# One feed-forward of layer 0 for the latent and the context tokens together

## The chip, the cores and the metric

The kernel runs on one core of a Trainium2 chip. The metric is the device time of one execution in microseconds (us). The engines are PE (TensorE, with its weight loads listed as PEld), DVE (VectorE), ACT (ScalarE), POOL (GpSimd) and SP (SyncE, which here issues most transfers). Lines such as L136 are lines of the kernel before.

## The reference, cut to what matters

Two blocks run one after the other. The first has two layers over 512 latent tokens (`x`) and 256 context tokens (`ctx`), 1024 features each; the second block, with an MLP in each of its two layers, works on the latent tokens alone. In layer 0 both streams pass through the same feed-forward with the same weights; in layer 1 only the latent stream does.

```
def conv_ffn(h, w_up, dw_w, dw_b, w_down):          # D_FF = 2816
    a, u = jnp.split(h @ w_up, 2, axis=-1)
    a = depthwise_conv(a, dw_w, dw_b)               # 3 taps along the tokens
    return (jax.nn.silu(a) * u) @ w_down
...
    x = layer_norm(ALPHA * x + ml[..., 2, :] * mix(zl, attn_l), ln1_g[l], ln1_b[l])
    x = layer_norm(ALPHA * x + ml[..., 5, :] * ffn(modulate(x, ml[..., 3, :], ml[..., 4, :])), ln2_g[l], ln2_b[l])
    if not last:                                    # layer 0 only
        ...
        ctx = layer_norm(ALPHA * ctx + mc[5] * ffn(modulate(ctx, mc[3], mc[4])), ln2_g[l], ln2_b[l])
```

`ml` and `mc` are six rows each, made from the conditioning vectors by a matrix `w_ada[l]` (`ada_mod`). The rows of layer 1 are needed from the end of layer 0 on.

## The kernel before

Every fp32 operand is kept as two halves, a rounded one (`hi`) and the rest (`lo`), and each product is three matmuls: hi x hi, hi x lo, lo x hi (`mm`, L153, L154, L155). A weight **unit** is 512 KB, 128 partitions by 1024 numbers. `unit` loads it on SP's queue into one of three `raw` buffers (L141), ACT rounds it into the `hi` half of a `w` buffer (L135), and DVE or POOL subtracts to get `lo` (L136). There are six `w` buffers; of every twelve units, `pool_share` go to POOL. Activations are cut in the same way by `split`, on buffers of tag `s8`.

The feed-forward (`ffn`) takes the 22 blocks of 128 hidden features, j, in three groups, (0,8), (8,16), (16,22). For each j, `up` multiplies two units (the `a` half and the `u` half) with all tokens, each into a PSUM bank of its own (tag `mm`, three banks). The activation follows: ACT copies `a` into a padded row (L1019), DVE does the three taps (L1021, L1024), ACT the tanh (L1027), DVE the products (L1028, L1029) and the cut into halves. After a group, `down` multiplies the group's features into the output tiles of 128 tokens, two halves of 512 features each. In the last group `tm_pair` finishes a tile at a time: scaling by the gate and sum (L1047 to L1049), then `ln_finish` (L581 to L600): on DVE the modulated rows h for the next stage (L591, L592, L595), and later (`residual`) on ACT and POOL the normalized rows that go to memory (L598 to L600). PE turns h into features by transposes (L310), and ACT and DVE cut them.

In layer 0, the mix of the latent stream ends with the product with `w_out` (`out_ln`) and writes its h to memory (`h_dram`, buffer `hd["l0"]`). Then the feed-forward of the context stream runs, woven with the first four of the twelve steps of `ada_vec` (rows of layer 1; DVE multiplies weight tiles with the conditioning vector, L502 and L504, and PE sums over partitions, L484; its weight tiles use `w` buffers as well); half of the units are cut on POOL (`pool_share` 6). Before its last group the latent h is read back (`reload`). The context's result goes to memory (`hd["c1"]`). Then the feed-forward of the latent stream runs, woven with the other eight steps, all units cut on DVE; its h stays on chip. The keys of layer 1 (`kv`) come next, and read the context's h back. `weave` takes steps of its generators by their rates; the order on each engine then follows a scheduler of the framework, which places instructions as their inputs and buffers are expected.

## Time and profile before

| | us |
|---|---|
| median of 3 runs | 4060.96 |
| lowest, highest | 4060.53, 4068.85 |
| the profiled execution | 4057.85 |
| its span, first to last instruction | 4056.1 |

| engine | busy, us | share of the span |
|---|---|---|
| PE | 3785.9 | 93% |
| DVE | 2729.4 | 67% |
| ACT | 1535.6 | 38% |
| POOL | 1059.9 | 26% |

The mean granted TensorE clock was 0.969 of full speed. The transfers moved 471.54 MB. A group of the profile's lines gives busy time, the mean of one instruction, and the idle time before these instructions with what ended it. Durations of neighbouring instructions overlap a little, so a pace is read from start to start.

### The profile page before, as it was taken

The page shows a single profiled execution, that of the slowest core. Times are in us where ns is not written, and L with a number is a line of the kernel's source. Part 1 is how long each engine was busy: PE and PEld are TensorE (multiplying, and loading weights), DVE is VectorE, ACT ScalarE, POOL GpSimd, SP SyncE. Part 2 cuts the span into 40 slices and gives each one's busy share as a digit, 9 for nine tenths or more (in the row PEclk, how much of TensorE's full clock was granted, in tenths as well). Part 3 has the DMA queues.
Part 4 walks back from the last instruction along what each step waited for, and adds up shares of the span by engine and source line. Part 5 has one row for each costly group of instructions (what it writes and reads, how often), then busy time and mean ns, then how long its engine had stood idle before and what let it go on. Part 6 is the DMA issues. An engine that isn't in the chain of part 4 may idle for free.

```text
span 4056.1 us, 49639 instructions
## 1 busy us (share of the span) xinstructions
PE 3785.9 (93%) x18765; PEld 3128.9 (77%) x18765; DVE 2729.4 (67%) x3713; ACT 1535.6 (38%) x2685; POOL 1059.9 (26%) x1028
## 2 busy tenths in 40 slices
PE   7788999799889999999979999999999999999999
PEld 4678787577687878777767788889788888778887
DVE  4998699976889766879996754563354346764444
ACT  3535444234343332344324233233432225653233
POOL 3654421675444001432256300110000002420000
PEclk9889999899999999999989999999999999999999
DMA  6456312355566455322234423333233232023332
GB/s 204 118 144 210 100 52 88 112 149 164 167 210 199 157 156 166 128 76 60 75 94 122 133 94 104 116 126 98 80 97 99 83 107 77 16 81 102 98 94 94
DMA packets 545242, 471.54 MB, mean 116 GB/s; under 512 B 30870, under 2 KB 435966, under 8 KB 545002
## 3 DMA queue, kind: packets, MB, share of 16 engines
q1 hardware_dynamic: 544922, 468.10, 37.5%
q8 instruction: 147, 2.41, 0.2%
q14 instruction: 93, 0.76, 0.1%
q0 software_dynamic: 80, 0.26, 0.0%
HBM read 443.50 MB, written 24.80 MB: 115 GB/s over the span
## 4 chain that ended last, share of the span: by engine, by line
PE 60%; DVE 26%; DMA 5%; issue 4%; ACT 3%; POOL 2%; SPq 0%; ACTq 0%; POOLq 0%; DVEq 0%
PE mm L153 18%; PE mm L154 18%; PE mm L155 18%; DVE s L787 10%; DVE w L136 4%; DVE s L136 2%; DVE s L504 1%; DVE st L740 1%; DMA w<-in_w_ada 1%; ACT w L135 1%; DMA raw<-in_w_in 1%; PE acc L161 1%; PE b L1256 1%; PE b L310 1%; DVE t L1024 1%
## 5 line engine op out<-in xcount | busy, mean ns | idle before, releaser
L153 PE MATMUL mm<-s,w 128*128 128x512 f32 (+1 forms) x3072 | 1126.9, 369 | 75.3 <-ACT pad L1019 19.0
L154 PE MATMUL mm<-s,w 128*128 128x512 f32 (+1 forms) x3072 | 1119.9, 365 | 10.2 <-DVE s L136 10.2
L155 PE MATMUL mm<-s,w 128*128 128x512 f32 (+1 forms) x3072 | 1117.5, 364 | 2.2 <-DVE w L136 2.2
L135 ACT CAST w<-raw 128x1024 fp32r<-128x1024 f32 (+4 forms) x673 | 689.2, 1029 | 820.0 <-PE mm L155 411.2
L136 DVE TENSOR_TENSOR w<-raw,w 128x1024 fp32r<-128x1024 f32 (+3 forms) x517 | 667.5, 1295 | 293.7 <-ACT w L135 288.8
L153 PE MATMUL mm<-w,s 128*128 128x512 f32 (+2 forms) x1960 | 750.4, 384 | 11.9 <-ACT s L135 5.6
L153 PEld LDWEIGHTS mm<-s,w 128*128 128x128 f32 x3072 | 599.8, 196 | 188.0 <-ACT pad L1019 21.2
L154 PE MATMUL mm<-w,s 128*128 128x512 f32 (+2 forms) x1960 | 741.6, 379 | 1.3 <-DVE w L136 1.3
L155 PE MATMUL mm<-w,s 128*128 128x512 f32 (+2 forms) x1960 | 739.0, 379 | 1.3 <-DVE s L136 1.3
L154 PEld LDWEIGHTS mm<-s,w 128*128 128x128 f32 x3072 | 602.0, 196 | 94.2 <-DVE s L136 12.1
L155 PEld LDWEIGHTS mm<-s,w 128*128 128x128 f32 x3072 | 600.9, 196 | 89.9 <-DVE w L136 2.6
L787 DVE SCALAR_TENSOR_TENSOR s<-pad,cols,s 128x512 f32<-128x512 f32 (+1 forms) x690 | 578.8, 881 | 1.1
L136 POOL TENSOR_TENSOR w<-raw,w 128x1024 fp32r<-128x1024 f32 (+1 forms) x156 | 420.2, 2695 | 471.6 <-ACT w L135 463.0
L153 PEld LDWEIGHTS mm<-w,s 128*128 128x128 f32 x1960 | 370.3, 189 | 92.3 <-issue 14.2
L155 PEld LDWEIGHTS mm<-w,s 128*128 128x128 f32 x1960 | 370.1, 189 | 67.6 <-DVE s L136 2.6
L154 PEld LDWEIGHTS mm<-w,s 128*128 128x128 f32 x1960 | 370.5, 189 | 63.6 <-DVE w L136 2.7
L320 POOL TENSOR_SCALAR st<-st 128x1 f32<-128x1 f32 (+2 forms) x91 | 32.8, 360 | 1216.1 <-ACT s L1086 902.4
L1101 DVE TENSOR_TENSOR s<-s,mm 128x512 f32<-128x512 f32 x80 | 54.6, 685 | 172.2 <-PE mm L155 172.2
L136 DVE TENSOR_TENSOR s<-b,s 128x256 fp32r<-128x256 f32 (+2 forms) x224 | 119.6, 545 | 51.2 <-ACT s L135 50.3
L135 ACT CAST s<-b 128x256 fp32r<-128x256 f32 (+2 forms) x224 | 104.1, 474 | 123.2 <-DVE s L136 73.4
L1117 DVE TENSOR_TENSOR t<-t 128x512 f32<-128x512 f32 x64 | 44.3, 692 | 154.0 <-ACT t L1116 154.0
L504 DVE SCALAR_TENSOR_TENSOR s<-w,cond,s 128x512 f32<-128x512 f32 x112 | 101.0, 921 | 43.4 <-DMA w<-in_w_ada 43.0
(273 smaller groups left out, 4307.2 us busy)
## 6 DMA issues: line engine op xcount, KB each, us to landing
raw<-in_w_up SPq DMA_DIRECT2D x196, 512.0 KB
raw<-in_w_in SPq DMA_DIRECT2D x180, 512.0 KB
raw<-in_w_down SPq DMA_DIRECT2D x130, 512.0 KB
w<-in_w_ada SPq DMA_DIRECT2D x48, 512.0 KB
raw<-in_w_ada SPq DMA_DIRECT2D x32, 512.0 KB
s<-d SPq DMA_DIRECT2D x26, 512.0 KB
raw<-in_conv_pw_w SPq DMA_DIRECT2D x24, 512.0 KB
raw<-in_w_out SPq DMA_DIRECT2D x24, 512.0 KB
```

The costliest lines, as they stand in the source:

```text
L135: self.nc.scalar.copy(hi, src)
L136: (eng or self.nc.vector).tensor_sub(lo, src, hi.bitcast(F32))
L153: mm(out, lhsT=l[0], rhs=r[0], start=first, stop=False)
L154: mm(out, lhsT=l[0], rhs=r[1], start=False, stop=False)
L155: return mm(out, lhsT=l[1], rhs=r[0], start=False, stop=last)
L161: self.nc.tensor.matmul(out, lhsT=l, rhs=r, start=first and n == 0, stop=last and n == len(terms) - 1)
L310: self.pe_mark = nc.tensor.transpose(ps[:, c, :], src[:, (c0 + c) * P : (c0 + c + 1) * P], self.ident)
L504: nc.vector.scalar_tensor_tensor(out=v, in0=w, scalar=c, in1=v, op0=ALU.mult, op1=ALU.add)
L740: self.mark = nc.vector.reduce_max(out=s[:, 0:1], in_=S[:, :nkeys], axis=AX.X, negate=True)
L787: nc.vector.scalar_tensor_tensor(out=o, in0=pad[:, k : k + T], scalar=self.col("dww", 8 * k + j), in1=o, op0=ALU.mult, op1=ALU.add)
L1101: nc.vector.tensor_add(x(t)[:, cs], x(t)[:, cs], ps)
L1117: nc.vector.tensor_mul(r, r, r)
```

## The change

Layer 0 gets one feed-forward for both streams, `ffn_both`. Each unit of `w_up` and `w_down` is loaded and cut once and used for the context tokens, then for the latent tokens: 66 fewer unit loads (34.6 MB), casts and subtractions. There are six groups: (0,2), (2,6), (6,10), (10,14), (14,18), (18,22). The two products of the context share one PSUM bank (`both`); those of the latent stream have one each. `down` has six output tiles (two of the context, four of the latent stream), and the last group finishes all six, the context's first.

The latent h of the mix and the context's h at the end stay on chip (`h_feat`), so both memory buffers and both reloads go. All twelve steps of `ada_vec` are woven in, from the start, at a rate of 2; `pool_share` stays 0. For the whole kernel there are twelve `s8` buffers instead of eleven and five `w` buffers instead of six. The second layer's `ffn` now has the groups (0,9), (9,18), (18,22). `ln_prep` can share the rows g and b of another call. The activation is moved, unchanged, into `ffn_act`.

```diff
+ADAV = 2
...
-    BUFS = {"s8": 11, "s4": 6, "w": 6, "raw": 3, "t2": 4, "pad": 6, "st": 16, "row": 3, "fa": 2, "colst": 2, "br": 1}
+    BUFS = {"s8": 12, "s4": 6, "w": 5, "raw": 3, "t2": 4, "pad": 6, "st": 16, "row": 3, "fa": 2, "colst": 2, "br": 1}
...
-    def ln_prep(self, g, b, mod, gate):
-
-        nc = self.nc
-        t1 = self.sb([P, 2, D], F32, "s8")
-        gb, bb = t1[:, 0, :], t1[:, 1, :]
-        self.bcast(gb, g)
-        self.bcast(bb, b)
+    def ln_prep(self, g, b, mod, gate, like=None):
+
+        nc = self.nc
+        if like is None:
+            t1 = self.sb([P, 2, D], F32, "s8")
+            gb, bb = t1[:, 0, :], t1[:, 1, :]
+            self.bcast(gb, g)
+            self.bcast(bb, b)
+        else:
+            gb, bb = like["g"], like["b"]
...
+    def ffn_act(self, H, i, j, pa, pu, T):
+
+        nc = self.nc
+        pad = self.sb([P, T + 30], F32, "pad")
+        nc.gpsimd.memset(pad[:, 0:1], 0.0)
+        nc.gpsimd.memset(pad[:, T + 1 : T + 2], 0.0)
+        nc.scalar.copy(pad[:, 1 : T + 1], pa)
+        a = self.sb([P, 512], F32, "t2")[:, :T]
+        nc.vector.tensor_scalar(a, pad[:, 0:T], scalar1=self.col("fww", j), scalar2=self.col("fwb", j),
+                                op0=ALU.mult, op1=ALU.add)
+        for k in (1, 2):
+            nc.vector.scalar_tensor_tensor(out=a, in0=pad[:, k : k + T], scalar=self.col("fww", 22 * k + j), in1=a,
+                                           op0=ALU.mult, op1=ALU.add)
+        th = self.sb([P, 512], F32, "t2")[:, :T]
+        nc.scalar.activation(th, a, AF.Tanh, scale=0.5)
+        nc.vector.scalar_tensor_tensor(out=a, in0=th, scalar=1.0, in1=a, op0=ALU.add, op1=ALU.mult)
+        nc.vector.tensor_mul(a, a, pu)
+        self.split(H.hi(i), H.lo(i), a)
+
+    def ffn_both(self, l, parts):
+
+        nc, A = self.nc, self.A
+        groups = [(0, 2), (2, 6), (6, 10), (10, 14), (14, 18), (18, 22)]
+        ys = [self.ytiles() for _ in parts]
+        sts = [[self.st() for _ in range(p[0].nt)] for p in parts]
+        tiles = [(q, t) for q, p in enumerate(parts) for t in range(p[0].nt)]
+        gate, bc = [], []
+        W1, W2 = A["w_up"][l], A["w_down"][l]
+
+        def add_prev(q, t, cs, ps, gi):
+            S, _, _, xin, _, _ = parts[q]
+            yt = ys[q](t)
+            if gi == 0:
+                nc.scalar.copy(yt[:, cs], ps)
+                return
+            nc.vector.tensor_add(yt[:, cs], yt[:, cs], ps)
+            if gi == len(groups) - 2:
+                xt = self.sb([P, 512], F32, "t2")
+                nc.sync.dma_start(xt, xin[t * P : t * P + P, cs])
+                nc.gpsimd.tensor_mul(yt[:, cs], yt[:, cs], gate[q][:, cs])
+                nc.vector.scalar_tensor_tensor(out=yt[:, cs], in0=xt, scalar=ALPHA, in1=yt[:, cs], op0=ALU.mult, op1=ALU.add)
+
+        def finish(q, t, n, ps):
+            S, _, mod, _, xout, h_out = parts[q]
+            yt, cs = ys[q](t), slice(n * 512, n * 512 + 512)
+            if len(bc) <= q:
+                bc.append(self.ln_prep(A["ln2_g"][l], A["ln2_b"][l], mod, None, bc[0] if bc else None))
+            v = self.sb([P, 512], F32, "t2")
+            nc.vector.tensor_mul(v, ps, gate[q][:, cs])
+            nc.vector.tensor_add(yt[:, cs], yt[:, cs], v)
+            nc.vector.bn_stats(out=sts[q][t][:, 6 * n : 6 * n + 6], in_=yt[:, cs])
+            return self.ln_finish(S, yt, t, sts[q][t], bc[q], xout, h_out) if n == 1 else None
+
+        for gi, (j0, j1) in enumerate(groups):
+            nk = j1 - j0
+            Hs = [Feat(self, p[0].T, nk) for p in parts]
+            for j in range(j0, j1):
+                us = [self.unit(W1[:, c : c + P], KD, P) for c in (j * P, DFF + j * P)]
+                for (S, X, *_), H in zip(parts, Hs):
+                    T = S.T
+                    if T <= 256:
+                        both = self.ps("mm")
+                        pss = [both[:, :T], both[:, T : 2 * T]]
+                    else:
+                        pss = [self.ps("mm")[:, :T] for _ in us]
+                    for u, ps in zip(us, pss):
+                        for k in range(KD):
+                            self.mm(ps, [u.part(hl, k, 0, P) for hl in (0, 1)], (X.hi(k), X.lo(k)), k == 0, k == KD - 1)
+                    self.ffn_act(H, j - j0, j, *pss, T)
+                yield
+            if gi == len(groups) - 2:
+                for p in parts:
+                    gate.append(self.sb([P, D], F32, "s4"))
+                    self.bcast(gate[-1], self.gate_row(l, p[0].s, 1))
+            last = gi == len(groups) - 1
+
+            def product(us, q, t):
+                tk = slice(t * P, t * P + P)
+                ps = self.ps("mm")
+                for k in range(nk):
+                    u, i = us[k]
+                    self.mm(ps, (Hs[q].hi(k)[:, tk], Hs[q].lo(k)[:, tk]), [u.part(hl, i, 0, 512) for hl in (0, 1)],
+                            k == 0, k == nk - 1)
+                return ps
+
+            if not last:
+                for n in range(2):
+                    us = self.tm_units(W2, 512 * n, 512, j0, nk)
+                    for q, t in tiles:
+                        add_prev(q, t, slice(512 * n, 512 * n + 512), product(us, q, t), gi)
+                    yield
+                continue
+            us = [self.tm_units(W2, 512 * n, 512, j0, nk) for n in range(2)]
+            late = None
+            for q, t in tiles:
+                for n in range(2):
+                    f = finish(q, t, n, product(us[n], q, t))
+                self.call(late)
+                late = f
+                yield
+            self.call(late)
+        self.flush()
...
-        groups = [(0, 8), (8, 16), (16, 22)]
+        groups = [(0, 9), (9, 18), (18, 22)]
...
+                self.ffn_act(H, i, j0 + i, pa, pu, T)
...
-    mix(0, lat, Xl, kT, vs, LAT + CTX, True, net.mod_rows(0, 0, 1), x0, xd["lat", 0], h_dram(hd["l0"]),
+    Xf = Feat(net, LAT, KD)
+    mix(0, lat, Xl, kT, vs, LAT + CTX, True, net.mod_rows(0, 0, 1), x0, xd["lat", 0], h_feat(Xf),
         before_out=lambda: Xcf.append(reload(cx, xd["ctx", 0], net.mod_rows(0, 1, 1))), extra=net.ada(0, 6, 12))
     if stop == "mix0":
         return xd["lat", 0], xd["ctx", 0]
-    Xlf = []
-    net.pool_share = 6
-    weave((net.ffn(0, cx, Xcf[0], bc_of(0, cx, True), xd["ctx", 0], None, h_dram(hd["c1"]),
-                   before_last=lambda: Xlf.append(reload(lat, hd["l0"]))), 1),
-          (net.ada_vec(1, 0, 4), 0.75))
-    net.pool_share = 0
-    Xf = Xlf[0]
-    X1 = Feat(net, LAT, KD)
-    weave((net.ffn(0, lat, Xf, bc_of(0, lat, True), xd["lat", 0], xd["lat", 1], h_feat(X1)), 1),
-          (net.ada_vec(1, 4, 12), 1.25))
+    X1, Xc1 = Feat(net, LAT, KD), Feat(net, CTX, KD)
+    net.mods[1] = net.dram([2, 6, D])
+    weave((net.ffn_both(0, [(cx, Xcf[0], net.mod_rows(1, 1, 0), xd["ctx", 0], None, h_feat(Xc1)),
+                            (lat, Xf, net.mod_rows(1, 0, 0), xd["lat", 0], xd["lat", 1], h_feat(X1))]), 1),
+          (net.ada_vec(1, 0, 12), ADAV))
     if stop == "ffn0":
-        return xd["lat", 1], hd["c1"]
+        return xd["lat", 1], None
 
     net.load_cols(1)
     net.gains(1)
     kT, Vc = keys(1)
-    vs = lat_keys(1, X1, kT, Vc, reload(cx, hd["c1"]))
+    vs = lat_keys(1, X1, kT, Vc, Xc1)
```

On PE, at the end of the first context j after the mix. In the kernel before, the second product of that j (bank mm_8732) ends and the next j begins:

```order
L154 MATMUL mm_8732<-s_1299_8329,w_8704 128x256
L155 MATMUL mm_8732<-s_1299_8329,w_8704 128x256
L153 MATMUL mm_8782<-s_1298_8326,w_8774 128x256
L154 MATMUL mm_8782<-s_1298_8326,w_8774 128x256
L155 MATMUL mm_8782<-s_1298_8326,w_8774 128x256
```

The same place after the change (mm_8778 is the shared bank of the context, s_1340 the first cut features of the latent h, b_1352 and b_1353 the transposes of its last two tiles):

```order
L156 MATMUL mm_8778<-s_1297_8327,w_8775 128x256
L311 MATMUL b_1352_8711<-ident_66,s_1346_8651 128x128 x8
L311 MATMUL b_1353_8728<-ident_66,s_1351_8707 128x128 x8
L154 MATMUL mm_8842<-s_1340_8630,w_8770 128x512
L154 MATMUL mm_8843<-s_1340_8630,w_8775 128x512
L155 MATMUL mm_8842<-s_1340_8630,w_8770 128x512
```

Before, another context j follows; after, two transposes and the latent products of the same j with the same two units.

On DVE, at the same place. In the kernel before, from the normalization of the last tile of the mix (st_8670) on:

```order
L581 BN_AGGR st_8670<-st_8352 128x2
L1024 SCALAR_TENSOR_TENSOR t_1357_8761<-pad_8757,cols_343,t_1357_8761 128x256
L591 SCALAR_TENSOR_TENSOR s_1347_8674<-s_1321_8464,st_8670,s_1257_8019 128x1024
L502 TENSOR_SCALAR s_1370_8847<-w_8848,cond_88 128x512 x2
L1028 SCALAR_TENSOR_TENSOR t_1357_8761<-t_1358_8765,t_1357_8761 128x256
L592 SCALAR_TENSOR_TENSOR s_1343_8634<-s_1343_8634,st_8630,s_1257_8019 128x1024
L595 SCALAR_TENSOR_TENSOR st_8630<-st_8630 128x1
L504 SCALAR_TENSOR_TENSOR s_1370_8847<-w_8848,cond_88,s_1370_8847 128x512 x2
L1029 TENSOR_TENSOR t_1357_8761<-t_1357_8761,mm_8732 128x256
```

After the change, from the second half of that normalization (s_1351 is the last tile's h, t_1367 the first context activation, s_1376 a sum of `ada_vec`):

```order
L596 SCALAR_TENSOR_TENSOR s_1351_8707<-s_1351_8707,st_8703,s_1255_8017 128x1024
L599 SCALAR_TENSOR_TENSOR st_8703<-st_8703 128x1
L137 TENSOR_TENSOR w_8927<-raw_8925,w_8927 128x1024
L137 TENSOR_TENSOR s_1342_8636<-b_1352_8711,s_1342_8636 128x2x128
L505 SCALAR_TENSOR_TENSOR s_1376_8907<-w_8914,cond_88,s_1376_8907 128x512 x2
L1026 SCALAR_TENSOR_TENSOR t_1367_8831<-t_1368_8835,t_1367_8831 128x256
L137 TENSOR_TENSOR s_1343_8639<-b_1352_8711,s_1343_8639 128x2x128
L137 TENSOR_TENSOR s_1340_8630<-b_1353_8728,s_1340_8630 128x2x128
L1027 TENSOR_TENSOR t_1367_8831<-t_1367_8831,mm_8778 128x256
L137 TENSOR_TENSOR s_1341_8633<-b_1353_8728,s_1341_8633 128x2x128
L137 TENSOR_TENSOR s_1369_8839<-t_1367_8831,s_1369_8839 128x256
```

The cuts of the transposed latent h (b_1352, b_1353) now stand here, between the context activation and the `ada_vec` sums.

On DVE, in the last group, as a tile is finished. In the kernel before, the third latent tile (s_1783 is its sum, s_2032 to s_2035 are cut features of the tiles before it):

```order
L1047 TENSOR_TENSOR t_2037_13580<-mm_13561,s_1894_12593 128x512
L136 TENSOR_TENSOR s_2033_13552<-b_2031_13540,s_2033_13552 128x2x128
L1048 TENSOR_TENSOR s_1783_11773<-s_1783_11773,t_2037_13580 128x512
L1049 BN_STATS st_11027<-s_1783_11773 128x6
L136 TENSOR_TENSOR s_2034_13555<-b_2031_13540,s_2034_13555 128x2x128
L1047 TENSOR_TENSOR t_2039_13603<-mm_13584,s_1894_12593 128x512
L136 TENSOR_TENSOR s_2035_13558<-b_2031_13540,s_2035_13558 128x2x128
```

After the change, from the middle of the group on (s_1400 and s_1403 are pairs of latent tiles, s_1902 and s_1909 the first two latent h, w_13522 a unit for the keys):

```order
L1059 TENSOR_TENSOR t_1918_13344<-mm_13331,s_1781_12271 128x512
L595 SCALAR_TENSOR_TENSOR s_1902_13234<-s_1400_9098,st_13230,s_1896_13202 128x1024
L595 SCALAR_TENSOR_TENSOR s_1909_13289<-s_1400_9098,st_13285,s_1896_13202 128x1024
L599 SCALAR_TENSOR_TENSOR st_13230<-st_13230 128x1
L1060 TENSOR_TENSOR s_1403_9115<-s_1403_9115,t_1918_13344 128x512
L599 SCALAR_TENSOR_TENSOR st_13285<-st_13285 128x1
L137 TENSOR_TENSOR w_13522<-raw_13520,w_13522 128x1024
L1059 TENSOR_TENSOR t_1923_13386<-mm_13373,s_1781_12271 128x512
L596 SCALAR_TENSOR_TENSOR s_1902_13234<-s_1902_13234,st_13230,s_1896_13202 128x1024
```

The normalization of the first two latent tiles stands behind the products of the third, and its cut features come later than that.

## Rows read from the trace of the kernel before

**Rows 1.** Page, costliest groups: busy, mean ns, then idle before and its releasers

```profile
L155 PE MATMUL mm<-s,w 128*128 128x512 f32 (+1 forms) x3072 | 1117.5, 364 | 2.2 <-DVE w L136 2.2
L135 ACT CAST w<-raw 128x1024 fp32r<-128x1024 f32 (+4 forms) x673 | 689.2, 1029 | 820.0 <-PE mm L155 411.2
```

**Rows 2.** Windows: busy (count) of PE PEld DVE ACT POOL; clock, DMA share, GB/s

```profile
1057.00:1307.00 250.00, 215.97 (x1369) 192.76 (x1370) 229.02 (x278) 96.29 (x150) 123.19 (x93) 0.94 0.65 204
1307.00:1647.00 340.00, 336.33 (x1454) 270.91 (x1453) 230.80 (x308) 105.56 (x137) 20.24 (x56) 0.99 0.52 164
1647.00:1735.00 88.00, 80.20 (x357) 62.12 (x355) 69.36 (x119) 31.64 (x69) 41.70 (x37) 0.96 0.26 87
...
2658.00:2720.00 62.00, 58.24 (x298) 49.28 (x297) 51.68 (x83) 25.59 (x50) 11.93 (x21) 1.00 0.48 152
```

**Rows 3.** Timeline of PE: start, duration, line; first products of five stages

```profile
1056.86 0.38 PE L153 MATMUL mm<-s,w 128*128 128x256 f32 x1
...
1306.90 0.39 PE L153 MATMUL mm<-s,w 128*128 128x512 f32 x1
...
1647.44 0.39 PE L153 MATMUL mm<-w,s 128*128 128x512 f32 x1
...
1692.50 0.77 PE L153 MATMUL mm<-w,s 128*128 128x512 f32 x1
...
1735.36 0.50 PE L153 MATMUL mm<-s,w 128*128 128x512 f32 x1
```

**Rows 4.** Timeline of PE: pace of 256 and of 512 columns

```profile
1114.83 0.28 PE L153 MATMUL mm<-s,w 128*128 128x256 f32 x1
1114.95 0.28 PE L154 MATMUL mm<-s,w 128*128 128x256 f32 x1
...
1377.31 0.50 PE L153 MATMUL mm<-s,w 128*128 128x512 f32 x1
...
1399.20 0.39 PE L153 MATMUL mm<-w,s 128*128 128x512 f32 x1
```

**Rows 5.** Lines of PE, 1012 to 1320 us

```profile
L153 PE MATMUL mm<-s,w 128*128 128x256 f32 x352 | 107.7, 306 | 30.3 <-ACT pad L1019 19.0 <-DVE t L1029 8.3 <-DVE s L1063 3.0
...
L484 PE MATMUL acc<-s,ones 128*1 128x512 f32 x16 | 8.2, 591 | 3.0 <-DVE t L485 3.0
```

**Rows 6.** Lines of DVE, 1320 to 1642 us (latent feed-forward)

```profile
L136 DVE TENSOR_TENSOR w<-raw,w 128x1024 fp32r<-128x1024 f32 x60 | 72.4, 1217 | 31.8 <-ACT w L135 31.7
L504 DVE SCALAR_TENSOR_TENSOR s<-w,cond,s 128x512 f32<-128x512 f32 x56 | 41.9, 747 | 39.2 <-DMA w<-in_w_ada 38.7
L1024 DVE SCALAR_TENSOR_TENSOR t<-pad,cols,t 128x512 f32<-128x512 f32 x42 | 31.4, 748 | 1.4
...
L1029 DVE TENSOR_TENSOR t<-t,mm 128x512 f32<-128x512 f32 x21 | 14.4, 684 | 1.5
...
L1021 DVE TENSOR_SCALAR t<-pad,cols 128x512 f32<-128x512 f32 x21 | 11.3, 538 | 1.6 <-ACT pad L1019 1.6
```

**Rows 7.** Lines of DVE and POOL, 1012 to 1320 us

```profile
L136 DVE TENSOR_TENSOR s<-b,s 128x256 fp32r<-128x256 f32 x16 | 6.3, 411 | 1.7 <-ACT s L135 1.7
...
L136 POOL TENSOR_TENSOR w<-raw,w 128x1024 fp32r<-128x1024 f32 x33 | 90.4, 2740 | 77.9 <-ACT w L135 71.1 <-DMA raw<-in_w_down 6.7
```

**Rows 8.** Timelines of DVE and POOL: one operation beside POOL and alone

```profile
1062.26 2.73 POOL L600 TENSOR_TENSOR s<-s,s 128x1024 f32<-128x1024 f32 x1
...
1062.65 2.48 DVE L1021 TENSOR_SCALAR t<-pad,cols 128x256 f32<-128x256 f32 x1
...
1101.69 0.40 DVE L1021 TENSOR_SCALAR t<-pad,cols 128x256 f32<-128x256 f32 x1
```

**Rows 9.** The same stage of layer 1: last mix product, last cut, first activation

```profile
2314.77 0.50 PE L181 MATMUL mm<-br,ones 32*128 32x512 f32 x1
...
2338.48 0.42 DVE L136 TENSOR_TENSOR s<-b,s 128x256 fp32r<-128x256 f32 x1 [0.44 <-ACT s L135]
```

**Rows 10.** Timeline of DVE: end of layer 0's last normalization

```profile
1702.69 1.28 DVE L592 SCALAR_TENSOR_TENSOR s<-s,st,s 128x1024 f32<-128x1024 f32 x1
```

More of the change, by code (lines that the diff above doesn't have):

```diff
@@ L1010, in ffn @@
         y = y or self.ytiles()
-        groups = [(0, 8), (8, 16), (16, 22)]
+        groups = [(0, 9), (9, 18), (18, 22)]
         def up(H, j0, j1):
             def cb(i, pa, pu):
-                j = j0 + i
-                pad = self.sb([P, T + 30], F32, "pad")
-                nc.gpsimd.memset(pad[:, 0:1], 0.0)
-                nc.gpsimd.memset(pad[:, T + 1 : T + 2], 0.0)
-                nc.scalar.copy(pad[:, 1 : T + 1], pa)
-                a = self.sb([P, 512], F32, "t2")[:, :T]
-                nc.vector.tensor_scalar(a, pad[:, 0:T], scalar1=self.col("fww", j), scalar2=self.col("fwb", j),
-                                        op0=ALU.mult, op1=ALU.add)
-                for k in (1, 2):
-                    nc.vector.scalar_tensor_tensor(out=a, in0=pad[:, k : k + T], scalar=self.col("fww", 22 * k + j), in1=a,
-                                                   op0=ALU.mult, op1=ALU.add)
-                th = self.sb([P, 512], F32, "t2")[:, :T]
-                nc.scalar.activation(th, a, AF.Tanh, scale=0.5)
-                nc.vector.scalar_tensor_tensor(out=a, in0=th, scalar=1.0, in1=a, op0=ALU.add, op1=ALU.mult)
-                nc.vector.tensor_mul(a, a, pu)
-                self.split(H.hi(i), H.lo(i), a)
+                self.ffn_act(H, i, j0 + i, pa, pu, T)
             return self.fm_gemm(X, A["w_up"][l], [(c * P, DFF + c * P) for c in range(j0, j1)], cb, lead=1 if lead and j0 == 0 else 0)
@@ L1641, in first_block @@
     xd = {(S.name, i): net.dram([S.T, D]) for S in (lat, cx) for i in range(3)}
-    hd = {k: net.dram([S.T, D]) for k, S in (("l0", lat), ("c1", cx))}
-    def h_dram(dst):
-        def f(t, h):
-            nc.sync.dma_start(dst[t * P : t * P + P, :], h)
-        return f
     def h_feat(X):
```

## Prediction

> **What bounds the kernel now.** I read the page first, then windows over the stretch that the change rewrites, then PE's timeline for its edges, and last the grouped lines of PE and DVE in it. PE is busy for 93% of the span, and weights are hardly ever what it waits for: its third matmul waited 2.2 us for a `lo` half in the whole run, while the casts stood idle 820 us, half of that until PE gave back a `w` buffer [rows 1]. So PE's own work sets the time, and 66 loads, casts and subtractions fewer are worth only what PE loses around them.
>
> What it loses is seen by pace. The stretch runs from the context's first product at 1056.86 to the first product behind the keys at 1735.36: 678.5 us [rows 3]. A matmul of 256 columns takes 0.12 us from start to start, one of 512 takes 21.89 / 96 = 0.228 [rows 4]. The context's `up` is 22 x 48 matmuls of 256 columns (126.7 us); the rest, 264 for its `down` and 1056 + 528 for the latent stream, has 512 (1848 x 0.228 = 421.3). That is 548. The keys take 1735.36 - 1692.50 = 42.9 with some 39 of work. The sums of `ada_vec` on PE take about 15: the context part holds half of them, with 8.2 us busy [rows 5]. The transposes of the reload take about 4 (an estimate: 32 of them at the size of a small matmul). So 678.5 - 548 - 39 - 15 - 4 = 72 us are lost, most of it in the context's 250 us (work 126.7 + 60.2 + 8 + 4 = 199, so 51 lost), where the granted clock was 0.94 [rows 2] and PE waited 30.3 us at the first matmul of a product, 19.0 of them for ACT's copy of the product before [rows 5]. Of the latent part up to its last group, 340.5 us, 328.3 are products and 7 sums: 5 lost. The last group and the keys together, 88 us, lose the other 16.
>
> **The change part by part.**
>
> *Matmuls.* The same 548 us of products, the same sums. The reload's transposes go (4 us saved); four tiles are now transposed out of the mix instead, two ahead of 1056.86 on PE and two behind it, so 2 + 2 us come back.
>
> *The start.* In the kernel before, the context's j follow each other and nothing needs the latent h for 250 us. Now the second thing PE does is the latent product of j = 0. Work that doesn't need it: 48 x 0.12 = 5.8 us of the context's j = 0 and 2 us of transposes, 7.8 us. The latent features are ready after a chain on DVE. By the order of the changed kernel some thirty operations stand between the last product of the mix and the first cut of its last tile: eleven cuts at 0.41 [rows 7] make 4.5; three unit subtractions at 1.2, six `ada_vec` sums at 0.75 [rows 6], two openings of a sum at about the same, two and a half normalizations at 1.28 for each half [rows 10], and small ones: about 21 us. With the hand-over to PE and POOL's work beside it I take 24.5. Layer 1 has this very stage already, with h kept on chip, and took 2338.90 - 2315.27 = 23.6 us from the last product to the last cut [rows 9]. So PE stands 24.5 - 7.8 = 17, and I add 2 for the lower clock after an idle time: 19 us (14 to 28).
>
> *The middle.* One j is 5.8 us of context and 48 x 0.228 = 10.9 of latent work: 16.7 us. On DVE one j has two unit subtractions (2.4), the latent activation (six operations of 0.54 to 0.75, about 3.7 as their starts overlap) and the context's (about 2.2 at half the width: 0.40 where the wide one has 0.54 [rows 6, 8]). `ada_vec` comes at two tiles a step, eight sums while both streams are conditioned (the first eight steps), 5.4 us start to start, then four. That is 13.9 us in 16.7 for those eight steps, 11 later. DVE has room, less than the latent part had (230.80 in 340 [rows 2]). The 33 subtractions of 2.74 us on POOL are gone [rows 7], and with them what they did to DVE: one tap took 2.48 us beside a POOL operation and 0.40 without [rows 8]. The shared bank makes ACT's copy of `a` wait for the `u` product, 24 x 0.12 = 2.9 us; behind it stand 10.9 us of latent work, which cover it. I take 12 us of stalls for the middle: twice the latent part's 5, for DVE's higher load. Bounds: 0, and 34, the context part's rate (51 in 250) over half of the 340 us.
>
> *The sum up to the last group:* before, 1647.44 - 1056.86 = 590.6. After: products without the last group 548 - 32.8 = 515.2, sums 15.2, transposes 4, start 19, middle 12: 565.5. Gain 25 us.
>
> *The tail.* Both kernels have 144 matmuls in the last group (8 x 18, now 12 x 12) and then the keys. But now six tiles are normalized instead of four, in the same 32.8 us of PE. A tile costs DVE two scalings, two sums and two statistics at 0.68, two passes at 1.28 and eight cuts at 0.41, partly joined: about 8.6 us, 52 for six against 33 of PE work. The keys' own 39 us follow, and take the latent tiles one by one with the context in between, so that most of it is covered. DVE's last cut comes about 73 us behind the group's start; the last tile's keys follow: 91.5 instead of 88, a loss of 3.5 (from a gain of 6, if the context's tiles are done under the latent products, to a loss of 17, two tiles in full).
>
> A rule of the Trainium skill (SBUF — State Buffer, "Who interferes with whom") speaks against this tail: VectorE and GpSimd share a port that is held for a whole instruction, and the later one waits. Rows 8 bear it out. The context's rows add four products and sums on POOL at 2.7 us and three for `ln_prep`, about 19 us: by the rule in full the tail would be 19 us longer, by the tail before, where POOL was busy 41.70 of 88 us and the loss was 16, hardly. I stay with 3.5.
>
> *Five `w` buffers.* PE waits for weights about 2 us now [rows 1]; one unit less of lead lets a late cast through here and there, in the mixes above all, where up to five units are live at once. Below by 0, above by 15 (as often as 30 units late by half a microsecond); I take 4.
>
> *Layer 1's groups.* The last group's products shrink from 32.8 to 21.9 us of PE, DVE's chain per tile stays. The last group's window before is 58.24 busy of 62 [rows 2], so the chain was nearly covered; 8.6 x 4 = 34 us of DVE now stand against 22. I take a loss of 4.5 (from -3 to +9).
>
> *Sum:* 25 - 3.5 - 4 - 4.5 = 13 us. The profiled execution took 4057.85 (span 4056.1), 3.1 less than the median 4060.96; so 4044.9 by its time, and 4048 by the median.
>
> **The rivals.**
>
> *A. More is recovered.* What is lost around the context goes nearly altogether: the start costs 12, as half of DVE's chain lies under the mix's last products, the middle 5 as in the latent part, and the five buffers and layer 1's groups cost nothing. Then 13 + 7 + 7 + 8.5 = 35 us: 4026. For it: PE is fully busy once a latent product is in the mix [rows 2]. Against: layer 1's 23.6 us at the same place [rows 9].
>
> *B. Nothing won.* The tail loses 17 as DVE sets its pace, the other terms stand: 4061.5. For it: DVE was busy 69.36 of the tail's 88 already [rows 2]. The Trainium skill's rule on the shared port, above, would bring about the same: 19 instead of 3.5, 4063.5.
>
> *C. Slower: `ada_vec` makes DVE the bound.* Its tiles share the five `w` buffers with the units, and DVE, which takes its work in order, waits for them: 39.2 us for 56 sums, so 2.8 us a tile [rows 6]. In the first eight steps two tiles cost up to 5.6 on top of 13.9, 19.5 against PE's 16.7; 2.8 us a step. The cuts of the units and of the features stand behind the waiting sums on DVE, and PE behind these. Eight steps make 22 us, which takes the place of nothing in the sum: 4070. It decides from 2.8 us of waiting in a step on. Against it: DVE could afford these waits in the latent part, as it had nothing else to do.
>
> *D. The saved traffic does nothing at all*, because PE bounds everything: then only the costs are left. The 51 us in the context part speak against it; it has no chance of its own beside B and C.
>
> **How the numbers follow.** The forecast 0.45 (alone 4036 to 4058), A 0.25, B 0.15, C 0.15. Range 4016 to 4072: A's side with some room below, as 72 us are there to be won, and C above. About 0.2% (8.1 us) is what a measurement of this kernel can tell. Faster than 4052.9: A whole, the forecast to four fifths, 0.62; slower than 4069.1: most of C and a little of the forecast's bounds, 0.17; the rest 0.21.
>
> **What would show it.** In the profile after: the time from the mix's last product to the first latent product without a gap, with 17 us idle on PE and the cuts of the last tile as releaser; 16.7 us per j with PE busy over 95% from there on; six latent and context tiles ending some 73 us behind the last group's first product; about 2 us more of waits for `w` halves in the mixes; layer 1's last group with idle time on PE. Wrong would be: steps longer than 17.5 us in the first eight with DVE waiting on `in_w_ada`, or a second layer or second block that takes over 10 us longer.

## The result and the profile after

The changed kernel is slower: 4085.62 us median (4083.25 to 4089.05) against 4062.28 for the kernel before on the same chip, a ratio of 1.0055 with an interval of 1.0038 to 1.0073. A gain of 13 us to 4048 was forecast, and 4072 was the upper end of the range. The profiled execution after took 4083.25 us (span 4081.2), that of before 4057.85, so the pair shows the loss (25 us). In the rows below, the lines of the changed kernel are numbered one or more higher (L136 is now L137, L153 to L155 are L154 to L156).

The first reading is a ledger by stage, from PE's timeline. The mixes end with the product of a bias row, which both kernels have; the second block begins with the first matmul of 320 columns.

| stage | before, us | after, us | difference |
|---|---|---|---|
| start to the end of layer 0's last mix | 1056.44 | 1072.39 | +16.0 |
| feed-forward of layer 0 and the keys | 678.50 | 668.86 | -9.6 |
| layer 1's mix | 579.83 | 582.82 | +3.0 |
| layer 1's feed-forward, to the second block | 395.11 | 406.96 | +11.9 |
| second block, to PE's end | 1337.13 | 1341.00 | +3.9 |

The edges that no other rows show, before and then after (start, duration):

```profile
1056.44 0.50 PE L181 MATMUL mm<-br,ones 32*128 32x512 f32 x1
...
1734.94 0.49 PE L181 MATMUL mm<-br,ones 32*128 32x512 f32 x1
...
2709.88 0.42 PE L153 MATMUL mm<-w,s 128*128 128x320 f32 x1 [0.42 <-ACT t L1142]
```

```profile
1072.39 0.49 PE L182 MATMUL mm<-br,ones 32*128 32x512 f32 x1
...
2324.07 0.49 PE L182 MATMUL mm<-br,ones 32*128 32x512 f32 x1
...
2731.03 0.30 PE L154 MATMUL mm<-w,s 128*128 128x320 f32 x1
```

The joint feed-forward did win time. What it won was lost in stages that it doesn't touch, and more. The first row needs care: ten executions of kernels with six `w` buffers ended that mix between 1056.44 and 1069.83, 1063.6 on average, and the profile of before that was shown is the earliest of them; the two kernels with five buffers ended it at 1072.39 and 1073.37. So about 9 of the 16 us are the kernel's, and the other stages lost some 28 us against the 9.6 won.

PE's timeline after, at the edges of the joint feed-forward (start, duration, operation, idle time before and what ended it), for comparison with [rows 3]:

```profile
1073.66 0.36 PE L154 MATMUL mm<-s,w 128*128 128x256 f32 x1
...
1096.35 1.94 PE L311 MATMUL b<-ident,s 128*128 128x128 f32 x8 [11.45 <-DVE st L599]
1098.75 1.22 PE L154 MATMUL mm<-s,w 128*128 128x512 f32 x2 [0.46 <-ACT s L136]
1104.36 0.79 PE L155 MATMUL mm<-s,w 128*128 128x512 f32 x1 [4.39 <-DVE s L137]
...
1156.79 0.28 PE L154 MATMUL mm<-s,w 128*128 128x256 f32 x1
...
1173.45 0.28 PE L154 MATMUL mm<-s,w 128*128 128x256 f32 x1
...
1637.45 0.39 PE L154 MATMUL mm<-w,s 128*128 128x512 f32 x1
...
1741.25 0.49 PE L182 MATMUL mm<-br,ones 32*128 32x512 f32 x1
```

The first context product comes at 1073.66, the first latent one at 1098.75, behind a transpose that waited 11.45 us for the normalization of the last tile. From 1156.79 to 1173.45 one j takes 16.66 us, as was worked out. The last group begins at 1637.45 and the keys end at 1741.25: 103.8 us. The same stretch before, from 1647.44 to 1734.94 (its bias row is shown above), took 87.5.

The windows show where PE stands (columns as in [rows 2]: busy and count of PE, PEld, DVE, ACT, POOL, then clock, DMA share, GB/s):

```profile
1073.00:1118.00 45.00, 25.07 (x134) 21.17 (x134) 40.99 (x54) 11.95 (x23) 19.19 (x12) 0.73 0.34 112
1118.00:1637.00 519.00, 514.37 (x2683) 429.72 (x2683) 335.56 (x517) 128.47 (x199) 26.76 (x98) 1.00 0.38 118
1637.00:1742.00 105.00, 84.15 (x356) 65.19 (x355) 84.65 (x134) 29.10 (x66) 51.73 (x43) 0.87 0.20 64
1676.00:1695.00 19.00, 5.19 (x21) 3.75 (x21) 19.00 (x17) 5.77 (x8) 12.53 (x4) 0.54 0.25 73
...
2680.00:2742.00 62.00, 51.70 (x257) 44.37 (x256) 48.65 (x80) 24.77 (x48) 13.07 (x21) 0.89 0.43 138
```

The middle, 519 us, is full (99% busy at full clock, 0.38 of the DMA engines against 0.65 and 0.52 in [rows 2]); the two ends are not. In the tail, the stretch from 1637.45 to 1741.25, there are 19 us in which DVE is busy without a gap and PE for 5.19, at a clock of 0.54. Layer 1's last group, the last line, has PE busy for 51.70 of 62 us at a clock of 0.89, where [rows 2] had 58.24 at 1.00.

And PE waits for weights, which it hardly did before [rows 1]. From the grouped lines of PE:

```profile
L156 PE MATMUL mm<-s,w 128*128 128x512 f32 (+1 forms) x3072 | 1115.7, 364 | 16.9 <-DVE w L137 12.4 <-POOL w L137 4.4
...
L460 PE MATMUL mm<-w,cw 128*4 128x512 f32 x128 | 34.0, 404 | 12.7 <-POOL w L137 10.2 <-DVE w L137 2.4
```

Over the whole run the waits of PE for a `lo` half of a weight come to 34.3 us, against 8.9 before. (3.3 of each stand ahead of a transpose in the second block, which uses no weight.) The timeline has nearly all of the rise at few places ahead of the feed-forward: two products with the conditioning vector (L460) and one of the context between 128 and 282 us, and six products between 731 and 857, the longest wait 6.05.

### The profile page after: what moved, and what is told of

The parts are those of the page before. It is cut to its first block, busy times and chain, and to the rows that moved or that the text cites. A ratio compares the mean times of both kernels' runs of the same rounds, so it can differ in the third digit from the quotient of the medians.

```text
span 4081.2 us, 49385 instructions
## 1 busy us (share of the span) xinstructions
PE 3792.8 (93%) x18765; PEld 3128.8 (77%) x18765; DVE 2667.9 (65%) x3718; ACT 1474.2 (36%) x2621; POOL 977.8 (24%) x995
## 4 chain that ended last, share of the span: by engine, by line
PE 64%; DVE 23%; issue 4%; DMA 3%; ACT 3%; POOL 2%; SPq 0%; POOLq 0%; ACTq 0%; DVEq 0%
PE mm L154 19%; PE mm L155 19%; PE mm L156 19%; DVE s L791 10%; DVE w L137 3%; DVE s L137 2%; DVE st L744 1%; DMA w<-in_w_ada 1%; PE acc L162 1%; PE b L1348 1%; ACT w L136 1%; PE b L311 1%; DVE s L505 1%; POOL w L137 1%; PE b L1550 1%
## 5 line engine op out<-in xcount | busy, mean ns | idle before, releaser
L154 PE MATMUL mm<-s,w 128*128 128x512 f32 (+1 forms) x3072 | 1121.2, 367 | 64.2 <-DVE t L897 20.6
L156 PE MATMUL mm<-s,w 128*128 128x512 f32 (+1 forms) x3072 | 1115.7, 364 | 16.9 <-DVE w L137 12.4
L155 PE MATMUL mm<-s,w 128*128 128x512 f32 (+1 forms) x3072 | 1118.0, 364 | 10.0 <-DVE s L137 10.0
L136 ACT CAST w<-raw 128x1024 fp32r<-128x1024 f32 (+5 forms) x609 | 621.7, 1024 | 797.7 <-PE mm L156 442.0
L137 DVE TENSOR_TENSOR w<-raw,w 128x1024 fp32r<-128x1024 f32 (+4 forms) x486 | 620.1, 1279 | 275.5 <-ACT w L136 267.6
L154 PE MATMUL mm<-w,s 128*128 128x512 f32 (+2 forms) x1960 | 750.3, 385 | 13.5 <-DVE s L137 4.1
L155 PE MATMUL mm<-w,s 128*128 128x512 f32 (+2 forms) x1960 | 740.3, 379 | 1.3 <-DVE w L137 1.3
L156 PE MATMUL mm<-w,s 128*128 128x512 f32 (+2 forms) x1960 | 735.7, 379 | 1.2 <-DVE s L137 1.2
L154 PEld LDWEIGHTS mm<-s,w 128*128 128x128 f32 x3072 | 596.7, 195 | 168.8 <-DVE t L897 22.6
L156 PEld LDWEIGHTS mm<-s,w 128*128 128x128 f32 x3072 | 597.6, 195 | 107.6 <-DVE w L137 15.3
L155 PEld LDWEIGHTS mm<-s,w 128*128 128x128 f32 x3072 | 598.6, 195 | 95.8 <-DVE s L137 11.8
L154 PEld LDWEIGHTS mm<-w,s 128*128 128x128 f32 x1960 | 371.0, 189 | 103.6 <-issue 18.2
L137 POOL TENSOR_TENSOR w<-raw,w 128x1024 fp32r<-128x1024 f32 x123 | 327.8, 2667 | 443.4 <-ACT w L136 439.6
L156 PEld LDWEIGHTS mm<-w,s 128*128 128x128 f32 x1960 | 370.6, 189 | 66.1 <-DVE s L137 2.3
L155 PEld LDWEIGHTS mm<-w,s 128*128 128x128 f32 x1960 | 371.4, 190 | 64.7 <-DVE w L137 2.5
L321 POOL TENSOR_SCALAR st<-st 128x1 f32<-128x1 f32 (+2 forms) x91 | 34.2, 376 | 1190.8 <-ACT s L1178 895.1
L136 ACT CAST s<-b 128x256 fp32r<-128x256 f32 (+2 forms) x224 | 104.4, 474 | 168.1 <-DVE s L137 84.5
L137 DVE TENSOR_TENSOR s<-b,s 128x256 fp32r<-128x256 f32 (+2 forms) x224 | 120.0, 546 | 51.1 <-ACT s L136 50.3
```

Source lines behind the costliest of these rows:

```text
L136: self.nc.scalar.copy(hi, src)
L137: (eng or self.nc.vector).tensor_sub(lo, src, hi.bitcast(F32))
L154: mm(out, lhsT=l[0], rhs=r[0], start=first, stop=False)
L155: mm(out, lhsT=l[0], rhs=r[1], start=False, stop=False)
L156: return mm(out, lhsT=l[1], rhs=r[0], start=False, stop=last)
```

## The experiments

Of each edit the lines that matter are shown. All ratios are to the kernel before, which ran in between on the same chip, with 95% intervals. "Tail" is the stretch from the last group's first product to the end of the keys of layer 1, "start" the time from layer 0's mix's last bias row to the 48th latent product of the joint feed-forward.

**Five buffers in the kernel before.**

```diff
-    BUFS = {"s8": 11, "s4": 6, "w": 6, ...
+    BUFS = {"s8": 11, "s4": 6, "w": 5, ...
-        groups = [(0, 8), (8, 16), (16, 22)]
+        groups = [(0, 9), (9, 18), (18, 22)]
```

> The kernel before with five w buffers instead of six, all else kept; the last group of a feed-forward holds six units at once with six j, so its three feed-forwards get the groups (0,9),(9,18),(18,22). Theory (the buffer costs the time in the mixes): the end of layer 0's mix, 1056.4 before, moves by +12 to +16 us, the layer-1 mix loses another 2 to 4; with the three regrouped feed-forwards +30 to +45 in all, so about 4095 to 4105 us. Rival (the mixes lost time because the latent h stayed on chip and the twelfth s8 buffer changed the order): the mix of layer 0 ends within 3 us of before, and only the regrouped feed-forwards cost, +15 to +30. My forecast of 4 us for the buffer in the whole kernel falls if the first holds.

Measured: 4114.58 us, 1.0110 (1.0095 to 1.0125). The mix ended at 1073.37, 17 us after the profile of before, but only some 10 after the mean of the ten. The partner, with the same groups and six buffers:

> The kernel before with six w buffers and the groups (0,9),(9,18),(18,22) in all three feed-forwards, the partner of the run with five buffers, which took 1.011 of the kernel before. Theory (the fifth buffer costs over 15 us by itself): 1.004 to 1.006 of before, so 20 us or more of the 45 are the buffer's. Rival (the groups cost most of it, the buffer the 4 us that I forecast): 1.009 to 1.010.

Measured: 4095.87 us, 1.0068 (1.0053 to 1.0083). So the buffer alone is worth 0.0042, 17 us, give or take some 8; the groups of three feed-forwards cost the other 28, more than I expected of them. The rival's 4 us for the buffer lie outside that interval. The theory holds at its lower edge: over 15 us by the middle of the interval, but 1.0068 where 1.004 to 1.006 was expected. By stage, the two profiles differ by 11.8 us at the end of layer 0's mix, 9.5 in layer 0's feed-forwards and keys, 2.2 in layer 1's feed-forward and 2.6 in the second block. Layer 1's mix, from which 2 to 4 us were expected, took 581.4 us with five buffers and 581.9 with six. The two kernels' third matmuls, with five buffers and with six:

```profile
L155 PE MATMUL mm<-s,w 128*128 128x512 f32 (+1 forms) x3072 | 1120.2, 365 | 22.0 <-DVE w L136 17.5 <-POOL w L136 4.5
```

```profile
L155 PE MATMUL mm<-s,w 128*128 128x512 f32 (+1 forms) x3072 | 1115.7, 364 | 0.6 <-POOL w L136 0.6
```

All waits for `lo` halves of weights together: 42.1 us with five, 7.9 with six. These waits are not the loss one for one, as the windows of the worst stretch show, with five and with six (columns as above):

```profile
720.00:870.00 150.00, 112.94 (x418) 76.11 (x417) 136.51 (x137) 45.29 (x55) 100.96 (x58) 0.83 0.39 114
```

```profile
720.00:870.00 150.00, 117.42 (x468) 83.63 (x467) 145.42 (x136) 48.62 (x61) 96.56 (x61) 0.86 0.43 126
```

Some 21 us of waits for weights stand there with five buffers and 1.7 with six, but PE is idle for 37 us and 33: most of the new waits take the place of others. With the longer idle time the granted clock is lower, 0.83 against 0.86.

**Six buffers in the changed kernel.** The room comes from the sums of the two context tiles, which move from an `s8` buffer to two `s4` ones.

```diff
-    BUFS = {"s8": 12, "s4": 6, "w": 5, ...
+    BUFS = {"s8": 11, "s4": 6, "w": 6, ...
-        ys = [self.ytiles() for _ in parts]
+        ys = [self.ytiles() if p[0].nt > 2 else self.ytiles4() for p in parts]
```

> The changed kernel with six w buffers again and eleven s8: the sums of the two context tiles move to two s4 buffers, which makes the room. Layer 1's groups stay (0,9),(9,18),(18,22). Theory (buffer): the mixes get back 15 of the 15 us they had lost by the end of layer 0's mix and 2 to 4 in layer 1: 4062 to 4070 us. Rival (h on chip): the end of the mix stays 10 us or more behind the kernel before, 4078 to 4088.

Measured: 4065.54 us, 0.9996 (0.9987 to 1.0006), 0.0059 or 24 us (give or take 8) less than the changed kernel, and near the middle of the theory's range. The mix got back 9.7 us and not 15: it ended at 1062.71. Another 6.3 came from the joint feed-forward ahead of its last group (558.8 instead of 565.1), 1.3 from layer 1's mix and 4.1 from the second block. This edit moves three things at once (the `w` buffer, the `s8` buffer and the place of the context's sums), so what the buffer costs alone is shown by the pair before.

**Layer 1's groups.** First in the kernel before, for that layer alone (`if l`), then back in the version above.

> The kernel before with the groups (0,9),(9,18),(18,22) in layer 1's feed-forward alone. Theory (a last group with 22 us of PE work no longer covers some 34 us of DVE work for its four tiles): nothing changes before 2658 us, and the stage behind it ends 10 to 13 us later, 4071 to 4075 us. Rival (the groups cost the 4.5 us that I forecast, and the rest of the 14 us lost there came with five buffers): +3 to +6 us.

Measured: 4076.12 us, 1.0019 (1.0010 to 1.0029), 7.7 us; the feed-forward with the start of the second block took 405.3 instead of 395.1. Between the two theories in the median, at the first one's number in the trace. The first product of the last group and the first matmul of 320 columns, before and with the new groups:

```profile
2658.24 0.39 PE L153 MATMUL mm<-w,s 128*128 128x512 f32 x1
```

```profile
2681.66 0.39 PE L153 MATMUL mm<-w,s 128*128 128x512 f32 x1
...
2732.55 0.30 PE L153 MATMUL mm<-w,s 128*128 128x320 f32 x1
```

With 96 products instead of 144, the last group and what follows it take 50.9 us instead of 51.6. The 48 products that moved ahead of it cost 10.9 us there, and nothing came back for them: this end is set by something else than PE's products.

> As the run before it, with layer 1's groups (0,8),(8,16),(16,22) again, which six buffers allow. Theory: a further 10 to 14 us, 4050 to 4058: faster than the kernel before by 4 to 12, what the joint feed-forward itself wins. Rival (groups cheap): a further 3 to 6 only.

Measured: 4054.98 us, 0.9972 (0.9960 to 0.9984), 9.8 us less than with the new groups, and that stage took 396.2 us again. The waits for weights of this version, from PE's lines:

```profile
L156 PE MATMUL mm<-s,w 128*128 128x512 f32 (+1 forms) x3072 | 1114.3, 363 | 0.0
...
L460 PE MATMUL mm<-w,cw 128*4 128x512 f32 x128 | 31.5, 395 | 1.6 <-POOL w L137 1.6
```

**The tail.** The other experiments build on this version, whose tail still takes 102.6 us.

```diff
         def residual():
             nc.scalar.activation(y, y, AF.Identity, scale=rs, bias=mv[:, 3:4])
-            nc.gpsimd.tensor_mul(y, y, bc["g"])
-            nc.gpsimd.tensor_add(y, y, bc["b"])
+            if not self.bare:
+                nc.gpsimd.tensor_mul(y, y, bc["g"])
+                nc.gpsimd.tensor_add(y, y, bc["b"])
```

> The version with six w buffers and layer 1's old groups, with the two POOL products of the latent residual rows left out in the joint feed-forward (eight operations; the rows then go to memory without gain and offset, so this output is not the reference's). From the first product of the last group to the end of the keys it took 102.6 us, against 88 in the kernel before. Theory (POOL's operations hold DVE up: from 1664 to 1679 us of that run four DVE operations took 2.8 to 3.4 us instead of 0.7 to 1.3): 10 to 14 us shorter, 89 to 93. Rival (the six normalizations of DVE themselves, and their order, set the end): 98 to 103.

Measured: one execution, 4047.69 us; the tail 92.8, 9.7 less, just below the theory's 10 to 14 and far from the rival. POOL's timeline and DVE's in the changed kernel (with six buffers the four operations below take the same), then the same place without POOL's products:

```profile
1679.65 5.96 POOL L603 TENSOR_TENSOR s<-s,s 128x1024 f32<-128x1024 f32 x2 [4.41 <-ACT s L602]
1685.57 6.62 POOL L604 TENSOR_TENSOR s<-s,s 128x1024 f32<-128x1024 f32 x2
...
1680.62 2.78 DVE L596 SCALAR_TENSOR_TENSOR s<-s,st,s 128x1024 f32<-128x1024 f32 x1
1683.32 3.37 DVE L137 TENSOR_TENSOR w<-raw,w 128x1024 fp32r<-128x1024 f32 x1
1686.61 3.36 DVE L596 SCALAR_TENSOR_TENSOR s<-s,st,s 128x1024 f32<-128x1024 f32 x1
...
1690.50 2.77 DVE L137 TENSOR_TENSOR w<-raw,w 128x1024 fp32r<-128x1024 f32 x1
```

```profile
1668.61 1.28 DVE L597 SCALAR_TENSOR_TENSOR s<-s,st,s 128x1024 f32<-128x1024 f32 x1
1669.80 1.22 DVE L138 TENSOR_TENSOR w<-raw,w 128x1024 fp32r<-128x1024 f32 x1
1670.93 1.28 DVE L597 SCALAR_TENSOR_TENSOR s<-s,st,s 128x1024 f32<-128x1024 f32 x1
...
1672.73 1.21 DVE L138 TENSOR_TENSOR w<-raw,w 128x1024 fp32r<-128x1024 f32 x1
```

Four operations (L596 and L137, twice each) take 12.3 us beside POOL and 5.0 without. The Trainium skill has a rule for this (SBUF — State Buffer, "Who interferes with whom"): whichever of the two comes first has the shared port for its whole instruction. These rows agree with it: DVE's L137 of 1683.32 ends at 1686.69, 1.1 us behind POOL's second L603 (1685.61), and without POOL it takes 1.22 in all.

Part of the 9.7 us has another cause. POOL also makes the inverse root of each normalization (L321, L322), and for the last latent tile it stood behind POOL's products; DVE waited for it:

```profile
1709.92 1.28 DVE L596 SCALAR_TENSOR_TENSOR s<-s,st,s 128x1024 f32<-128x1024 f32 x1 [2.72 <-POOL st L322]
```

Without the products this wait is gone. By these rows some 7 us are longer operations and 2.7 a wait in POOL's queue.

```diff
-            for q, t in tiles:
+            for q, t in sorted(tiles, key=lambda a: -a[0]):      # last group
-CTXAT = 2
+CTXAT = 4
```

> The same version with the four latent tiles first and the two context tiles last in the last group, and the keys in that order too. Theory (the order of the six tiles matters, since the latent normalization waits behind the context's on DVE and for its rows of modulation): the 102.6 us from the last group to the end of the keys fall by 5 to 10 us. Rival (DVE's sum of work and POOL's collisions set it, in whatever order): within 3 us.

Measured: 4041.71 us, 0.9946 (0.9928 to 0.9964); the tail 97.1, 5.5 less: the lower edge of the theory. Both together:

> The version with the latent tiles first, with the POOL products of the joint feed-forward's latent residual rows left out. Leaving them out took 9.7 us from the tail of 102.6, the order 5.5. Theory (two separate causes): the tail is 87 to 89 us, as long as before the change. Rival (the new order had only moved the collisions): 92 to 94.

Measured: one execution, 4041.05 us; the tail 89.6. Just above the theory's 87 to 89 and below the rival's 92 to 94: of 9.7 + 5.5, 13.0 are left when both are done. The whole is hardly shorter than the profiled execution with the order alone (4041.32): the 7.5 us that this tail won were lost again behind it, 3.9 of them in layer 1's feed-forward. Whether that is chance, one execution can't tell.

**The start.**

```diff
-          (net.ada_vec(1, 0, 12), ADAV))
+          (after(2, net.ada_vec(1, 0, 12)), ADAV))      # skips two turns
```

> The same version with ada_vec starting one step later (two of its steps skipped at the start), so that its sums leave the chain of DVE between the mix's last product and the first latent product. From the mix's last bias product to the end of the first latent j it lost some 24 us. Theory (DVE's chain sets the start): 4 to 6 us shorter there, as six to eight sums of 0.75 go; in all -4, some 4051. Rival (the transposes wait for the normalization, whose own chain is not longer without the sums): within 1 us.

Measured: 4053.25 us, 0.9960 (0.9947 to 0.9973), and the start 42.5 instead of 43.6. No test of the theory: two openings and six sums still stood in DVE's chain, since the order places them as soon as their tiles are there. With ten turns skipped, on the version with the latent tiles first:

> The version with the latent tiles first (six w buffers, 0.9946 of the kernel before) with ada_vec starting five steps later, ten of its steps skipped. The run that skipped two had left six of its operations in DVE's chain at the start, so it told little. Here the first sum stands behind the first latent cuts on DVE. Theory (the sums lengthen that chain): the 48th latent product comes 5 to 7 us sooner than the 43.9 us behind the mix's end that it took, and the whole is 4 to 7 us shorter, some 4036. Rival (POOL's operations and the normalization itself set the start): within 1.5 us.

Measured: 4035.51 us, 0.9923 (0.9907 to 0.9940). The start fell from 43.9 to 37.1 us, as the theory said, and the whole by 6 (by the ratios 9, give or take 10). This version beats both kernels: 32 us under the one before, which took 4067.34 beside it.

> The same kernel with the POOL products of the latent residual rows at the end of layer 0's mix left out (eight operations; the rows go to memory without gain and offset, and all that follows is computed from them). Theory (POOL's operations hold DVE up in the start as in the tail: beside them two normalization passes took 3.4 and 2.5 us instead of 1.3 and two sums 5.3 instead of 1.4): the 48th latent product comes another 4 to 8 us sooner. Rival (the chain of the last tile is as long without them): within 1.5 us.

Measured: one execution, 4025.47 us; the start 27.6, another 9.6 less, more than the 4 to 8 of the theory. In the changed kernel DVE has no idle time from 1072 to 1104, so here its operations set the chain, and not a wait for an inverse root. The same wait of PE, for the last tile's transposes, without POOL's products and with them:

```profile
1073.87 1.72 PE L312 MATMUL b<-ident,s 128*128 128x128 f32 x8 [3.74 <-DVE s L597]
```

```profile
1083.31 1.94 PE L311 MATMUL b<-ident,s 128*128 128x128 f32 x8 [8.96 <-DVE st L599]
```

## Why the prediction was wrong

- **Up to the last group: right as a sum, in part by luck.** From the mix's end it was to take 565.5 us, and took 565.1 (591.0 before). Its parts were off in opposite ways. The start lost some 24 us, not 19 (within 14 to 28): of 44.9 us to the 48th latent product, about 20 are work. To DVE's 21 us of operations I had added 3.5 for the hand-over and for POOL's work beside them; without the sums in that chain, POOL's products alone cost 9.6. The middle lost 6 to 7, not 12. And 6.3 of the 565.1 us came with the fifth buffer, which was a term of its own: with six buffers this part took 558.8.
- **Five `w` buffers: the step that failed.** I took 4 us, at most 15. The pair of kernels before gives 17, the pair of changed kernels 24 (with the `s8` buffer and the sums moved as well), and PE's waits for weights rise from 7 or 8 us to 34 or 42. I had read "PE waited 2.2 us" as distance from a limit. The other row of [rows 1] spoke against it: the casts stood 411 us waiting for PE to give back a buffer. At those times all buffers were full, so their number was the whole lead, and where units are used up faster than they are made, the lead is what PE lives on. The rows of PE's waits agree with this at 731 to 857 us, though most of these waits took the place of others; I had spread the loss over 30 places of half a microsecond.
- **The tail: the second step that failed.** 3.5 us were taken, on the view that the keys' work covers DVE's, and it lost 16.3 (103.8 against 87.5), the end of my bounds (17, rival B's term). The last six tiles keep DVE busy without a gap for 19 us, and there POOL's products lengthen DVE's operations, and later its wait for an inverse root: 9.7 us. The order, context first, costs 5.5. My price of 19 for the port rule was near by luck, as it was worked out wrongly: the context's rows go nowhere in this layer, so POOL got only three operations more, those of `ln_prep`. The eight latent products were there before; that DVE sets the time beside them only now is argued, as the kernel before was not run without them.
- **Layer 1's groups: mis-sized.** 4.5 were taken; 7.7 and 9.8 were measured in two kernels, around the upper bound of 9. PE's last group of 22 us against 34 of DVE fits what was seen: the end of that stage did not get shorter with its products. The granted clock there also fell, from 1.00 to 0.89, which I had left out.
- **Rival C was wrong in a telling way.** In the middle DVE did wait for the tiles of `in_w_ada`, 58 us in all, and of the fifteen j that another j follows directly (from 1156.79 on), eleven took 16.66 us. Three took 17.7 to 18.3, just above my sign of 17.5, with two sums of `ada_vec` on PE in each:

```profile
L505 DVE SCALAR_TENSOR_TENSOR s<-w,cond,s 128x512 f32<-128x512 f32 x98 | 71.7, 747 | 58.7 <-DMA w<-in_w_ada 58.0
```

  DVE was busy for 335.56 of 519 us there; these waits lay in time that it had.
- **Sum.** 26 up to the last group, -16 tail, -9 first mix (against the mean of the ten), -3 layer 1's mix, -12 its feed-forward (some 10 of them the groups) and -4 second block give -18; the pair of profiles says -25, of which some 7 are the early mix of the profile before. The larger part of the miss is the price of the room that the change needed, one `w` buffer for one `s8` buffer. The groups of layer 1 belong to that price: with six j the last group holds six units at once. The rest is the tail.

Why five buffers cost 24 us in one pair and 17 in the other stays open; the intervals overlap.

## What to carry to other kernels

When a large part of a producer's idle time ends by a buffer given back (half of it here), the pool is often full and its size is the lead. What one buffer less costs can't be read from how long the consumer waits today, nor from how its waits for that buffer grow; a run with one buffer less, in the kernel before, tells it. A last group that ends in a normalization should be sized by the engine with the longer chain, with operations at the length that they have beside their neighbours. And a win in one stage has to be checked against what its buffers take from all others: with the room found elsewhere, the same joint feed-forward made the kernel faster by 0.3%, and by 0.8% with two changes of order.

## What the runs showed of the hardware

Even an operation on one column waits for POOL. In the changed kernel DVE's L599 took 0.13 to 0.16 us in 14 of 16 places, and 2.33 and 2.35 in two, both beside a product of POOL:

```profile
1658.55 3.17 POOL L575 TENSOR_TENSOR s<-s,s 128x1024 f32<-128x1024 f32 x1
...
1659.38 2.35 DVE L599 SCALAR_TENSOR_TENSOR st<-st 128x1 f32<-128x1 f32 x1
```

After the idle stretch in the tail, PE's matmuls of 512 columns come every 0.43 us, at the lower of its two clocks (1.2 GHz), and later again every 0.23. Ahead of it PE had been busy for 5.19 of 19 us:

```profile
1695.53 0.63 PE L155 MATMUL mm<-w,s 128*128 128x512 f32 x1
1695.95 0.63 PE L156 MATMUL mm<-w,s 128*128 128x512 f32 x1
1696.38 0.63 PE L154 MATMUL mm<-w,s 128*128 128x512 f32 x1
...
1704.02 0.39 PE L154 MATMUL mm<-w,s 128*128 128x512 f32 x1
1704.25 0.39 PE L155 MATMUL mm<-w,s 128*128 128x512 f32 x1
```

And executions of the same instructions differ: up to the end of layer 0's mix, the kernel with layer 1's new groups has the same operations in the same order on PE, DVE, ACT and POOL as the kernel before, and ended that mix 13.4 us later (1069.83 against 1056.44).
